# An encoder layer on one core: attention output stored in two halves, keys split over 128 partitions, value products recorded later

## The chip, the cores and the metric

One Trainium2 chip; the program runs on 1 of its cores. The metric is the device time of one execution in microseconds (us), lower is better. The engines are named as the profile names them: PE (TensorE) multiplies matrices, PEld is its weight load, ACT (ScalarE) and DVE (VectorE) work element by element, POOL (GpSimd) does a few small steps, SP (SyncE) issues every DMA. Each engine runs its own list of instructions in order and waits on semaphores.

## The reference, cut to what matters

One layer: three branches from one input projection, merged, then a feed-forward part with a convolution. Only the first branch is touched: stick-breaking attention, 16 heads of 64, 1024 prompt tokens and 64 sample tokens behind 256 cached ones, all float32.

```python
def _sb_block(qb, k, v, q_pos):
    mask = k_pos[None, :] < q_pos[:, None]
    z = einsum('bhqd,bhkd->bhqk', qb, k) * (SB_HEAD_DIM ** -0.5)
    log_beta = log_sigmoid(z)
    log_1mb = where(mask, log_sigmoid(-z), 0.0)
    excl = cumsum(log_1mb, axis=3, reverse=True) - log_1mb
    a = where(mask, exp(log_beta + excl), 0.0)
    return einsum('bhqk,bhkd->bhqd', a, v)
# in the layer
o_sb = stick_breaking(q, concat(k_past, k), concat(v_past, v), past_len)
y_sb = o_sb.transpose(0, 2, 1, 3).reshape(b, t, SB_WIDTH) @ w_sb_o
merged = sigmoid(ga) * y_sb + sigmoid(gb) * y_conv + sigmoid(gc) * y_mem
```

## The kernel before

Every large product keeps float32 accuracy with three passes of reduced-width matmuls: an operand x is split into a rounded part `hi` (written by ACT) and the rest `lo = x - hi` (written by DVE); `split` is these two instructions. Work runs in stages: memory keys and values; input projections with the convolution; then the attention stage of this case; three output projections (`mo` for memory, `cv` for convolution, `sb` for attention); the merged output projection; the feed-forward part.

**Attention stage.** Heads go in 8 pairs p = 0 to 7, a head of a pair is i = 0 or 1. `project(p)` makes q, k and v of a pair, each a dense product of 24 steps of three matmuls. Behind it runs the attention of pair p-1, cut into units: unit (p, i, c) holds queries 256c to 256c+255 (order c = 0, 2, 1, 3), and a sample unit closes each head. A unit makes scores `z` (PE, q in hi and lo against k stored as hi in 64 partitions and lo in the other 64), two sigmoids `be` and `r` (ACT), a scan of `r` and a product (DVE), and then for each block b of 256 keys a *turn* (four PE transposes into `aT`, split into `ath` by ACT and `atl` by DVE) and *values* (four matmuls of `ath` and `atl` against `vp`, whose 128 columns hold hi and lo of v). So one half of the 128 rows of the result `av` comes from v's hi part and the other from its lo part; their sum is the head's output. It is made here: ACT copies one half to `tmp` (L849), DVE adds the other to `os` (L851), and `os` goes to the DRAM tensor `d_os`.

**Order on PE.** PE's list is the order in which the code is recorded. `Weave.mix` lets one step of the projection pass and then asks `take` for a piece of attention that is due by a planner's clock `now`: values first (due 3.4 after their turn), then late transposes, turns, scores. No third turn is taken while two turned blocks wait for their values. At the start of `project(p)` for p > 1, `weave.until` records all that is left of pair p-2, due or not, piece after piece, with no projection step between. ACT, DVE and SP lists are set by a scheduler that places instructions by its own model. Buffers are handed out in the order of that model; `av` is one PSUM bank, `row` has four buffers.

**Output projection.** `project_out(1, ...)` runs `cv` for 8 column blocks m, then `project_out(0, ...)` runs `sb`. `sb` reads its operand as 8 rows of 128 channels: `sb_rows` loads rows 0 to 2 of `d_os` during the last `cv` block, the loop behind it the others; each is split into `sbh` and `sbl`. Block m = 0 of `sb` takes the 8 rows in turn, nine matmuls each. Gates (`cvg`, `sbg`) are loaded into the same four `row` buffers.

Of the kernel before, what the change touches and what calls it, by code (L numbers as in the profile page):

```python
# [8 lines left out]
F32 = mybir.dt.float32  # L9
F32R = mybir.dt.float32r  # L10
# [7 lines left out]
P = 128  # L18
# [32 lines left out]
def encoder_step(ctx: ExitStack, tc: tile.TileContext, I, O):  # L51
# [33 lines left out]
    d_silu = dp.tile([D, T], F32, name="d_silu")  # L85
    d_om = dp.tile([D, T], F32, name="d_om")
    d_os = dp.tile([D, T], F32, name="d_os")
    d_mg = dp.tile([D, T], F32, name="d_mg")
    d_x1 = dp.tile([T, D], F32, name="d_x1")

# [568 lines left out]
    with ExitStack() as st:  # L659
# [9 lines left out]
        def project(p, S):  # L669
# [62 lines left out]
            S["ks"], S["kc"] = ks, kc  # L732

            def k_split(dst, ps, c):
                for i in range(2):
                    a = slice(64 * i, 64 * i + 64)
                    b = slice(64 - 64 * i, 128 - 64 * i)
                    ACT.copy(out=dst[i][a, c], in_=ps[a, :])
                    DVE.tensor_tensor(out=dst[i][b, c], in0=ps[a, :], in1=dst[i][a, c].bitcast(F32), op=ALU.subtract)

            def evac_k(ps, t0, n):
                token_major(ps, t0, n, "k", O["sb_k_prompt"], O["sb_k_sample"])
# [39 lines left out]
        def unit(p, S, i, c):  # L782

            hr = slice(64 * i, 64 * i + 64)
            qd, ql, ks = S["qd"][i], S["ql"][i], S["ks"][i]
            bes, scores, rest = [], [], []

            def score(tb, gi, k0, m, cell):
                q = slice(tb * P, (tb + 1) * P)
                n = P * (tb + 1)  # L790
                if gi == 0:
                    tg = "s" if tb < 4 else ""
                    wd = 512 if tb < 4 else 1024
                    be = ap.tile([P, wd], F32, tag="be" + tg, name=f"be{p}{i}{tb}", bufs=4)
                    cell.append(ap.tile([P, wd], F32, tag="r" + tg, name=f"r{p}{i}{tb}", bufs=2))
                    bes.append(be)
                z = bank("z", f"z{p}{i}{tb}_{k0}")
                kk = slice(k0, k0 + m)
                PE.matmul(z[:, :m], qd[:, q], ks[:, kk], start=True, stop=False)
                dg = k0 <= tb * P < k0 + m  # L800
                PE.matmul(z[:, :m], ql[:, q], ks[:, kk], start=False, stop=not dg)
                if dg:
                    o = tb * P - k0
                    PE.matmul(z[:, o : o + P], identb, maskb, start=False, stop=True)
                be, r = bes[-1], cell[0]
                stick(P, [(z, k0, min(m, n - k0))], n, be, r)
                if k0 + m >= n:
                    sticks(P, n, be, r)

            for tb in (2 * c, 2 * c + 1):  # L810
                cell = []
                for gi, (k0, m) in enumerate(ZG[tb + 1]):
                    scores.append(lambda a=(tb, gi, k0, m, cell): score(*a))

            split_of = {}
            acc = []

            def turn(b):
                tp = bank("tr", f"aT{p}{i}{c}{b}")
                hi = ap.tile([P, 512], F32R, tag="ath", name=f"ath{p}{i}{c}{b}", bufs=2)  # L820
                lo = ap.tile([P, 512], F32R, tag="atl", name=f"atl{p}{i}{c}{b}", bufs=2)
                if b < c:
                    for a in range(2):
                        for e in range(2):
                            o = a * 256 + e * P
                            PE.transpose(tp[:, o : o + P], bes[e][:, (2 * b + a) * P : (2 * b + a + 1) * P], ident)
                    split(hi, lo, tp)
                    order = ((2 * b, 0, 0), (2 * b + 1, 0, 256))
                else:
                    PE.transpose(tp[:, 0:P], bes[1][:, (2 * c + 1) * P : (2 * c + 2) * P], ident)  # L830
                    for e in range(2):
                        PE.transpose(tp[:, (1 + e) * P : (2 + e) * P], bes[e][:, 2 * c * P : (2 * c + 1) * P], ident)  # L832
                    split(hi[:, 0:384], lo[:, 0:384], tp[:, 0:384])
                    order = ((2 * c, 0, P), (2 * c + 1, P, 0))
                split_of[b] = (hi, lo, order)

            def values(b):
                if b == 0:
                    acc.append(bank("av", f"av{p}{i}{c}"))
                av = acc[0]  # L840
                hi, lo, order = split_of.pop(b)
                for j, t0, o in order:
                    n = 256 - t0
                    PE.matmul(av[:, t0:256], S["vp"][i][:, j, :], hi[:, o : o + n], start=j == 0, stop=False)
                    PE.matmul(av[:, t0:256], S["vp"][i][:, j, :], lo[:, o : o + n], start=False, stop=j == 2 * c + 1)
                if b == c:
                    tmp = ap.tile([P, 256], F32, tag="tmp", name=f"tmp{p}{i}{c}", bufs=1)
                    ot = slice(64 - 64 * i, 128 - 64 * i)
                    ACT.copy(out=tmp[hr, :], in_=av[ot, :256])  # L849
                    os_ = ap.tile([P, 256], F32, tag="os", name=f"os{p}{i}{c}", bufs=2)  # L850
                    DVE.tensor_tensor(out=os_[hr, :], in0=av[hr, :256], in1=tmp[hr, :], op=ALU.add)  # L851
                    SP.dma_start(out=d_os[p * P + 64 * i : p * P + 64 * i + 64, 256 * c : 256 * c + 256], in_=os_[hr, :])

            n = P * (2 * c + 2)
            return Unit(scores, [lambda b=b: turn(b) for b in range(c + 1)], [lambda b=b: values(b) for b in range(c + 1)], n)
# [53 lines left out]
        class Weave:  # L909
# [23 lines left out]
            def take(self, force=False):  # L933

                if self.vq and (force or (self.vq[0][0] <= self.now and (self.vq[0][1] is self.summed or self.v_at + 2.6 <= self.now))):
                    _, u, f, last = self.vq.pop(0)
                    self.summed, self.v_at = u, self.now
                    f()
                    self.valued += 1
                    u.over = last  # L940
                    return self.PIECE
                if self.lq and (force or (self.lq[0][0] <= self.now and self.t_at[-2] + 2.6 <= self.now)):
                    self.lq.pop(0)[1]()
                    self.t_at.append(self.now)
                    return 0.33
                if self.tq and self.turned - self.valued < 2:
                    at, u, f, last = self.tq[0]
                    if force or (at <= self.now and self.t_at[-2] + 2.6 <= self.now):
                        self.tq.pop(0)
                        f()  # L950
                        self.t_at.append(self.now)
                        self.turned += 1
                        self.vq.append((self.now + 3.4, u, u.values[0], last))
                        u.values.pop(0)
                        if last:
                            self.done.append(u)
                        return self.PIECE
                if self.zq:
                    u, f, last = self.zq[0]
                    free = len(self.open) < 3 or u in self.open  # L960
                    if free and (force or (self.zq_ready <= self.now and self.z_at[-2] + 2.2 <= self.now)):
                        self.zq.pop(0)
                        if u not in self.open:
                            self.open.append(u)
                        f()
                        self.z_at.append(self.now)
                        if last:
                            for i, g in enumerate(u.turns):
                                self.tq.append((self.now + u.scan, u, g, i == len(u.turns) - 1))
                        return self.PIECE  # L970
                return 0.0
# [36 lines left out]

        def ap_tile(kind, shape, name):
            tag, bufs, w = {  # L1010
                "c": ("be", 4, 1024), "q": ("r", 2, 1024), "s": ("os", 2, 256), "v": ("tmp", 1, 256), "d": ("sf", 1, 192)
            }[kind]
            return ap.tile([P, w], F32, tag=tag, name=name, bufs=bufs)[:, : shape[1]]

# [123 lines left out]
    with ExitStack() as st:  # L1138
# [35 lines left out]

        sb_raw = []

        def sb_rows(m):
            if m == NK - 1:
                sb_raw.extend(row(d_os[k * P : (k + 1) * P, :], f"sbr{k}") for k in range(3))

        project_out(1, cv_ops, "cv", sb_rows, lambda m: None)
        sb_ops = act_rows("sb")
        for k in range(NK):
            raw = sb_raw[k] if k < len(sb_raw) else row(d_os[k * P : (k + 1) * P, :], f"sbr{k}")
            split(sb_ops[0][k], sb_ops[1][k], raw)
        project_out(0, sb_ops, "sb", lambda m: None, wo_load)

# [342 lines left out]
```

## Time and profile before

| | |
|---|---|
| median of 3 runs | 2532.03 us (2529.49 to 2532.94) |
| profiled execution | 2529.34 us, its span on the core 2527.5 us |
| PE busy | 2454.8 us, 97% of the span, 14639 matmuls |
| DVE busy / ACT busy | 1625.5 us (64%) / 1043.3 us (41%) |
| granted PE clock, mean | 0.998 |
| attention stage, 740 to 1380 us | PE busy 592.58 of 640 us, DVE 503.08, ACT 407.72 |
| DMA in all | 224.84 MB, mean 89 GB/s |

The span runs from the first to the last instruction; about 2 us of the execution lie around it. Since PE is busy nearly throughout and its list is fixed, the time is the sum of PE's work and of the stretches in which PE waits; the views that say where it waits are the table of waits by engine, the table of busy time by stage and the instructions in order of time.

### The profile page before, as it was taken

Reading aid. Unit: us, or ns where it says so; the run is one execution under the profiler, and the core shown is the slowest. Engines: PE = TensorE matmul, PEld = TensorE weight load, DVE = VectorE, ACT = ScalarE, POOL = GpSimd, SP = SyncE. Lnnn points to the kernel's source line nnn. Section 1 sums busy time; section 2 is a strip of 40 time slices with the busy share of each in tenths; the row PEclk is TensorE's granted clock in tenths of the full one; section 3 lists DMA queues with packets and bytes.
Section 4 is the critical chain, followed back from the end, with each engine's and each line's share of the span. In section 5 each row is a group of like instructions: output and inputs, shape, how many; then the busy total and the mean of one; then the engine's idle time right before and its main releaser. Section 6 shows DMA issues by size and latency. Waiting matters only on the chain. (4 is left out here: it accounts for less than half of the span.)

```text
span 2527.5 us, 36086 instructions
## 1 busy us (share of the span) xinstructions
PE 2454.8 (97%) x14639; PEld 2321.6 (92%) x14639; DVE 1625.5 (64%) x1963; ACT 1043.3 (41%) x2031; POOL 97.6 (4%) x301
## 2 busy tenths in 40 slices
PE   8999999999899999999989999999999999999998
PEld 6999999999898888888879999979999999999997
DVE  6687878787758777788786435444545444454456
ACT  7224142424656666566664203144223332222243
POOL 1000000000000000000000000011000000000001
PEclk9999999999999999999999999999999999999999
DMA  7322222222552322322343546122111110110114
GB/s 264 93 66 82 73 83 69 69 92 69 178 157 67 81 69 56 79 66 65 99 132 119 182 162 198 60 92 84 51 51 51 51 51 26 50 51 26 51 42 151
DMA packets 256055, 224.84 MB, mean 89 GB/s; under 512 B 58143, under 2 KB 227251, under 8 KB 255889
## 3 DMA queue, kind: packets, MB, share of 16 engines
q1 hardware_dynamic: 255889, 222.54, 29.3%
q8 instruction: 115, 1.88, 0.3%
q14 instruction: 51, 0.42, 0.1%
HBM read 153.22 MB, written 55.91 MB: 83 GB/s over the span
## 5 line engine op out<-in xcount | busy, mean ns | idle before, releaser
L93 DVE TENSOR_TENSOR wlo<-wraw,whi 128x1024 fp32r<-128x1024 f32 x156 | 190.3, 1220 | 280.5 <-ACT whi L92 277.9
L151 PE MATMUL up<-h2h,whi 128*128 128x362 f32 (+1 forms) x1056 | 348.2, 330 | 0.0
L152 PE MATMUL up<-h2l,whi 128*128 128x362 f32 (+1 forms) x1056 | 347.0, 329 | 0.0
L153 PE MATMUL up<-h2h,wlo 128*128 128x362 f32 (+1 forms) x1056 | 344.9, 327 | 0.0
L418 DVE SCALAR_TENSOR_TENSOR acc<-u,cw,acc 128x1118 f32<-128x1118 f32 x240 | 331.6, 1382 | 5.6
L92 ACT CAST whi<-wraw 128x1024 fp32r<-128x1024 f32 x156 | 164.3, 1053 | 302.3 <-PE cv L152 73.2
L1115 ACT COPY up<-up 128x364 f32<-128x364 f32 (+3 forms) x176 | 60.7, 385 | 352.0 <-PE up L153 352.0
L153 PEld LDWEIGHTS up<-h2h,wlo 128*128 128x128 f32 x1056 | 199.5, 189 | 0.0
L152 PEld LDWEIGHTS up<-h2l,whi 128*128 128x128 f32 x1056 | 198.6, 188 | 0.5
L151 PEld LDWEIGHTS up<-h2h,whi 128*128 128x128 f32 x1056 | 198.3, 188 | 0.4
L151 PE MATMUL g<-hh,whi 128*128 128x362 f32 (+1 forms) x576 | 190.4, 331 | 0.0
L153 PE MATMUL g<-hh,wlo 128*128 128x362 f32 (+1 forms) x576 | 189.2, 328 | 0.0
L152 PE MATMUL g<-hl,whi 128*128 128x362 f32 (+1 forms) x576 | 188.7, 328 | 0.0
L779 DVE TENSOR_TENSOR_SCAN r<-r 128x128 f32<-128x128 f32 (+7 forms) x128 | 171.8, 1350 | 25.4 <-ACT r L775 25.2
L1388 DVE TENSOR_TENSOR yacc<-yacc,dn 128x512 f32<-128x512 f32 x144 | 96.8, 686 | 82.6 <-PE dn L1375 62.2
L1107 DVE SCALAR_TENSOR_TENSOR fa<-up,fw,fa 128x1090 f32<-128x1090 f32 (+2 forms) x92 | 119.8, 1302 | 5.8 <-ACT fa L1105 4.5
L93 DVE TENSOR_TENSOR atl<-aT,ath 128x512 fp32r<-128x512 f32 (+1 forms) x160 | 99.0, 632 | 31.5 <-ACT ath L92 29.8
L92 ACT CAST ath<-aT 128x512 fp32r<-128x512 f32 (+1 forms) x160 | 85.6, 552 | 72.1 <-PE aT L832 39.2
L1375 PE MATMUL dn<-wdh,gl 128*128 128x512 f32 x288 | 112.2, 389 | 0.0
L1374 PE MATMUL dn<-wdl,gh 128*128 128x512 f32 x288 | 112.1, 389 | 0.0
L1373 PE MATMUL dn<-wdh,gh 128*128 128x512 f32 x288 | 112.1, 389 | 0.0
L152 PEld LDWEIGHTS g<-hl,whi 128*128 128x128 f32 x576 | 108.6, 189 | 0.2
(405 smaller groups left out, 6318.9 us busy)
## 6 DMA issues: line engine op xcount, KB each, us to landing
wraw<-in_w_in SPq DMA_DIRECT2D x72, 512.0 KB
wraw<-in_w_ffn_up SPq DMA_DIRECT2D x44, 512.0 KB
d_gate<-gt SPq DMA_DIRECT2D x24, 544.0 KB
wdr<-in_w_ffn_down SPq DMA_DIRECT2D x22, 512.0 KB
wraw<-in_w_mem_kv SPq DMA_DIRECT2D x16, 512.0 KB
qd<-qd SPq DMA_DIRECT2D x24, 272.0 KB
ql<-ql SPq DMA_DIRECT2D x24, 272.0 KB
d_om<-ost SPq DMA_DIRECT2D x8, 544.0 KB
```

The lines of the kernel that those rows point to most:

```text
L92: ACT.copy(out=hi, in_=src)
L93: DVE.tensor_tensor(out=lo, in0=src, in1=hi.bitcast(F32), op=ALU.subtract)
L151: PE.matmul(ps, wh[:, k, :], rh[k][c], start=first, stop=False)
L152: PE.matmul(ps, wh[:, k, :], rl[k][c], start=False, stop=False)
L153: PE.matmul(ps, wl[:, k, :], rh[k][c], start=False, stop=last)
L418: DVE.scalar_tensor_tensor(out=acc, in0=u[:, t : t + 1118], scalar=cw[:, t * 8 + i : t * 8 + i + 1], in1=acc, op0=ALU.mult, op1=ALU.add,)
L779: DVE.tensor_tensor_scan(out=rv, data0=rv, data1=rv, initial=1.0, op0=ALU.mult, op1=ALU.min)
L1107: DVE.scalar_tensor_tensor(out=acc[:, a:b], in0=raw[:, a + t : b + t], scalar=fw[:, t * 44 + m : t * 44 + m + 1], in1=acc[:, a:b], op0=ALU ...
L1373: PE.matmul(y, gh[:, tt], wh[:, c], start=first, stop=False)
L1374: PE.matmul(y, gh[:, tt], wl[:, c], start=False, stop=False)
L1375: PE.matmul(y, gl[:, tt], wh[:, c], start=False, stop=last)
L1388: DVE.tensor_tensor(out=yacc[t][:, c], in0=yacc[t][:, c], in1=y, op=ALU.add)
```

## The change

Five edits, all around the attention stage.

1. **Output halves.** The add in the values step goes. ACT copies all 128 rows of `av` into `os` (L853 of the changed kernel), and two DMAs store the halves, one to `d_os`, one to a new DRAM tensor `d_ol`. When `sb` needs a row, `sb_row` loads it from both and DVE adds them (L1185). The second load takes a `row` buffer too, and two rows instead of three are loaded ahead.
2. **Key split.** `k_split` was two ACT copies and two DVE subtractions on 64 partitions each. It is now one `split` on 128 partitions, and three DMAs per chunk that carry the halves to their places. The third overwrites what the second reads.
3. **Values later.** The planner's delay from a turn to its values goes from 3.4 to 4.6.
4. **Buffers.** `be` of the long score rows: four buffers of 1024 become one of each width (640, 768, 896, 1024); `r`: two of 1024 become one of 896 and one of 1024.
5. **Layer norm tiles** of the one block (64 rows) left for this stage take the renamed buffers.

```diff
+    d_ol = dp.tile([D, TP], F32, name="d_ol")
             def k_split(dst, ps, c):
-                for i in range(2):
-                    a = slice(64 * i, 64 * i + 64)
-                    b = slice(64 - 64 * i, 128 - 64 * i)
-                    ACT.copy(out=dst[i][a, c], in_=ps[a, :])
-                    DVE.tensor_tensor(out=dst[i][b, c], in0=ps[a, :], in1=dst[i][a, c].bitcast(F32), op=ALU.subtract)
+                n = c.stop - c.start
+                hi = ap.tile([P, 384], F32R, tag="kh", name=f"kh{p}_{n}_{c.start}", bufs=3)
+                split(hi[:, :n], dst[1][:, c], ps)
+                up, dn = slice(0, 64), slice(64, P)
+                for out, src in ((dst[0][up, c], hi[up, :n]), (dst[0][dn, c], dst[1][up, c]), (dst[1][up, c], hi[dn, :n])):
+                    SP.dma_start(out=out.bitcast(F32), in_=src.bitcast(F32))
...
-                    be = ap.tile([P, wd], F32, tag="be" + tg, name=f"be{p}{i}{tb}", bufs=4)
-                    cell.append(ap.tile([P, wd], F32, tag="r" + tg, name=f"r{p}{i}{tb}", bufs=2))
+                    else:
+                        be = ap.tile([P, n], F32, tag=f"be{tb}", name=f"be{p}{i}{tb}", bufs=1)
+                        cell.append(ap.tile([P, P * (7 + tb % 2)], F32, tag=f"r{tb % 2}", name=f"r{p}{i}{tb}", bufs=1))
...
                 if b == c:
-                    tmp = ap.tile([P, 256], F32, tag="tmp", name=f"tmp{p}{i}{c}", bufs=1)
-                    ot = slice(64 - 64 * i, 128 - 64 * i)
-                    ACT.copy(out=tmp[hr, :], in_=av[ot, :256])
                     os_ = ap.tile([P, 256], F32, tag="os", name=f"os{p}{i}{c}", bufs=2)
-                    DVE.tensor_tensor(out=os_[hr, :], in0=av[hr, :256], in1=tmp[hr, :], op=ALU.add)
-                    SP.dma_start(out=d_os[p * P + 64 * i : p * P + 64 * i + 64, 256 * c : 256 * c + 256], in_=os_[hr, :])
+                    ACT.copy(out=os_, in_=av[:, :256])
+                    rows = slice(p * P + 64 * i, p * P + 64 * i + 64)
+                    for h, dst in enumerate((d_os, d_ol)):
+                        SP.dma_start(out=dst[rows, 256 * c : 256 * c + 256], in_=os_[64 * h : 64 * h + 64, :])
...
-                        self.vq.append((self.now + 3.4, u, u.values[0], last))
+                        self.vq.append((self.now + 4.6, u, u.values[0], last))
...
+        def sb_row(k):
+            raw = row(d_os[k * P : (k + 1) * P, :], f"sbr{k}")
+            low = op.tile([P, T], F32, tag="row", name=f"sbl{k}", bufs=4)
+            SP.dma_start(out=low[:, :TP], in_=d_ol[k * P : (k + 1) * P, :])
+            DVE.tensor_tensor(out=raw[:, :TP], in0=raw[:, :TP], in1=low[:, :TP], op=ALU.add)
+            return raw
...
-                sb_raw.extend(row(d_os[k * P : (k + 1) * P, :], f"sbr{k}") for k in range(3))
+                sb_raw.extend(sb_row(k) for k in range(2))
...
-            raw = sb_raw[k] if k < len(sb_raw) else row(d_os[k * P : (k + 1) * P, :], f"sbr{k}")
+            raw = sb_raw[k] if k < len(sb_raw) else sb_row(k)
```

How the lists move, at three places. A row names line, operation, output and inputs; in `aT2133` the digits are pair 2, head 1, unit 3, block 3, and `v3_2` is the third chunk of v of pair 3.

**PE, where the projections of pair 4 begin.** Before, the end of unit (2, 1, 3): steps of `v3_2` stand between a turn and its values, 20 rows from `aT2133` to `ath2133`.

```order
L830 MATMUL aT2133_9426<-ident_69,be217_9174 128x128
...
L153 MATMUL v3_2_9434<-hh3_113,wlo75_8878 128x320
L844 MATMUL av213_9385<-ath2132_9409,vp21_8310 128x256
...
L151 MATMUL v3_2_9434<-hh4_114,whi75_8877 128x320
...
L844 MATMUL av213_9385<-ath2133_9427,vp21_8310 128x256
...
L893 MATMUL avs21_9496<-sf21_9455,vpr2_7948 128x64 x2
L894 MATMUL avs21_9496<-sf21_9455,vn0_6354 128x64
L151 MATMUL q4_0_9509<-hh0_110,whi76_9230 128x384
```

Now the same place: v has ended, and what is left of the unit follows in one piece.

```order
L154 MATMUL v3_2_9392<-hh7_118,wlo75_8886 128x320
L849 MATMUL av213_9457<-ath2130_9397,vp21_8288 128x256
...
L831 MATMUL aT2132_9462<-ident_69,be217_9222 128x128
L849 MATMUL av213_9457<-ath2131_9417,vp21_8288 128x256
...
L849 MATMUL av213_9457<-ath2132_9463,vp21_8288 128x256
...
L706 MATMUL vT3_768_9483<-ident_69,vf3_768_9455 128x128 x2
...
L835 MATMUL aT2133_9499<-ident_69,be217_9222 128x128
...
L849 MATMUL av213_9457<-ath2133_9500,vp21_8288 128x256
...
L885 MATMUL asT21_9515<-ident_69,bes21_9304 128x128 x3
L897 MATMUL avs21_9521<-sf21_9519,vpr2_7956 128x64 x2
...
L152 MATMUL q4_0_9534<-hh0_111,whi76_9250 128x384
```

What moved: the values of blocks 1, 2 and 3 and of the sample, and the turns of blocks 2 and 3, from between steps of `v3` to behind its last one; block 2's values now have only block 1's between them and their turn, block 3's nothing. The same stands at the starts of `q2` to `q7`, six times; for pairs 0, 4 and 5 block 1's values have only block 0's between them and their turn as well, for pair 3 a step of v besides.

**ACT at the same place.** Before:

```order
L92 CAST ath2132_9409<-aT2132_9408 128x512
L699 COPY vf3_384_9420<-v3_1_9326 128x384
L92 CAST ath2133_9427<-aT2133_9426 128x384
L883 COPY sf21_9455<-asT21_9451 128x192
L849 COPY tmp213_9464<-av213_9385 64x256
L710 COPY vs3_384_9473<-vT3_384_9469 128x384
L92 CAST vp30_9228<-vT3_384_9469 128x3x64
L92 CAST vp31_9229<-vT3_384_9469 128x3x64
L699 COPY vf3_768_9490<-v3_2_9434 128x320
L92 CAST whi77_9503<-wraw77_9234 128x1024
L896 COPY oss21_9500<-avs21_9496 64x64
```

Now:

```order
L700 COPY vf3_768_9455<-v3_2_9392 128x320
L93 CAST whi77_9528<-wraw77_9254 128x1024
L93 CAST vp31_9249<-vT3_384_9440 128x3x64
L93 CAST ath2132_9463<-aT2132_9462 128x512
L711 COPY vs3_768_9487<-vT3_768_9483 128x256
L93 CAST vp30_9248<-vT3_768_9483 128x2x64
L93 CAST ath2133_9500<-aT2133_9499 128x384
L93 CAST vp31_9249<-vT3_768_9483 128x2x64
L721 COPY vs3_768_9487<-vT3_768_9483 64x128
L853 COPY os213_9511<-av213_9457 128x256
L887 COPY sf21_9519<-asT21_9515 128x192
L900 COPY oss21_9525<-avs21_9521 64x64
```

What moved: `ath2132` and `ath2133` stood ahead of the copies of v's last chunks and of the weight split `whi77`, which cannot start before v has ended; now they stand behind them.

**SP, the loads for `sb`.** Before (`wraw` and `wor` are weights, `sbg` gates):

```order
L1144 DMA sbr0_15174<-d_os_100 128x1088
L124 DMA wraw105_15184<-in_w_sb_o 128x8x128
L1144 DMA sbr1_15176<-d_os_100 128x1088
L124 DMA wraw106_15315<-in_w_sb_o 128x8x128
L1144 DMA sbr2_15178<-d_os_100 128x1088
L1172 DMA wor0_15398<-in_w_out 128x1024
L1144 DMA sbr3_15289<-d_os_100 128x1088
L1144 DMA sbr4_15293<-d_os_100 128x1088
L1144 DMA sbr5_15297<-d_os_100 128x1088
L124 DMA wraw107_15408<-in_w_sb_o 128x8x128
L1144 DMA sbr6_15301<-d_os_100 128x1088
L1144 DMA sbr7_15305<-d_os_100 128x1088
```

Now:

```order
L1148 DMA sbr0_15175<-d_os_100 128x1088
...
L1184 DMA sbl0_15177<-d_ol_101 128x1024
...
L1148 DMA sbr1_15180<-d_os_100 128x1088
L1184 DMA sbl1_15182<-d_ol_101 128x1024
L1176 DMA wor0_15423<-in_w_out 128x1024
L1148 DMA sbr2_15292<-d_os_100 128x1088
L1184 DMA sbl2_15294<-d_ol_101 128x1024
...
L1184 DMA sbl3_15301<-d_ol_101 128x1024
L1148 DMA sbr4_15306<-d_os_100 128x1088
...
L1184 DMA sbl7_15329<-d_ol_101 128x1024
...
L1148 DMA sbg0_15334<-d_gate0_94 128x1088
```

What moved: each of the eight rows is two loads, so the places that were taken by rows 1 and 2 while `cv` was still running are taken by the second half of row 0 and by row 1. A load waits until its buffer is free: `sbl1` for the end of the next to last `cv` block, `sbl2` for the add of row 1, `sbr3` for row 1's split, `sbl3` for the add of row 2, `sbl5` for row 3's split, `sbl7` for row 5's split.

More of the change, by code (lines that the diff above doesn't have):

```diff
@@ L791, in score @@
                 if gi == 0:
-                    tg = "s" if tb < 4 else ""
-                    wd = 512 if tb < 4 else 1024
-                    be = ap.tile([P, wd], F32, tag="be" + tg, name=f"be{p}{i}{tb}", bufs=4)
-                    cell.append(ap.tile([P, wd], F32, tag="r" + tg, name=f"r{p}{i}{tb}", bufs=2))
+                    if tb < 4:
+                        be = ap.tile([P, 512], F32, tag="bes", name=f"be{p}{i}{tb}", bufs=4)
+                        cell.append(ap.tile([P, 512], F32, tag="rs", name=f"r{p}{i}{tb}", bufs=2))
+                    else:
+                        be = ap.tile([P, n], F32, tag=f"be{tb}", name=f"be{p}{i}{tb}", bufs=1)
+                        cell.append(ap.tile([P, P * (7 + tb % 2)], F32, tag=f"r{tb % 2}", name=f"r{p}{i}{tb}", bufs=1))
                     bes.append(be)
@@ L1010, in ap_tile @@
             tag, bufs, w = {
-                "c": ("be", 4, 1024), "q": ("r", 2, 1024), "s": ("os", 2, 256), "v": ("tmp", 1, 256), "d": ("sf", 1, 192)
+                "c": ("be7", 1, 1024), "q": ("r1", 1, 1024), "s": ("os", 2, 256), "v": ("os", 2, 256), "d": ("sf", 1, 192)
             }[kind]
```

## The prediction

> **What bounds the kernel now.** I read the page's busy times, then busy time by stage, then PE's waits, then the instructions around them.
>
> ```profile
> PE 2454.8 (97%) x14639; PEld 2321.6 (92%) x14639; DVE 1625.5 (64%) x1963; ACT 1043.3 (41%) x2031; POOL 97.6 (4%) x301
> 740.00:1380.00 640.00, 592.58 (x3990) 551.38 (x3989) 503.08 (x700) 407.72 (x962) 0.54 (x1) 1.00 0.33 85
> 1380.00:1520.00 140.00, 140.00 (x849) 140.00 (x847) 52.58 (x76) 21.20 (x20) 0.00 (x0) 1.00 0.48 164
> 1520.00:1560.00 40.00, 40.00 (x245) 40.00 (x243) 28.31 (x36) 15.03 (x15) 0.00 (x0) 1.00 0.75 250
> PE av L845 <- DVE atl L93: 26.7, 23, 1.7
> PE z L799 <- ACT r L775: 10.0, 8, 1.3
> PE av L844 <- DVE os L851: 4.9, 9, 1.1
> PE vT L705 <- DVE vp L93: 3.3, 1, 3.3
> PE avs L893 <- DVE os L851: 1.3, 1, 1.3
> ```
>
> Columns of the stages: length, then busy time of PE, PEld, DVE, ACT, POOL, then clock and DMA. PE is the bound: it idles 47.4 us in the attention stage and not at all from 1380 on, where `cv` and `sb` run. The change leaves PE's matmuls as they are, so only waits count: it can win at most those of the attention stage, and whatever it makes PE wait after 1380 us is new. All five waits listed (total, times, longest) fall in that stage; four of them, 42.9 us, are what the change reaches.
>
> **The change part by part: the waits it removes.** The largest is for `atl`, the rest of a turned block. It comes 3 times per head pair, here the longest; and the wait of `z` is one stall of ACT:
>
> ```profile
> 859.98 0.39 PE L845 MATMUL av<-atl,vp 128*128 128x256 f32 x1 [1.64 <-DVE atl L93]
> 884.18 0.55 DVE L739 TENSOR_TENSOR ks<-k,ks 64x384 fp32r<-64x384 f32 x1
> 884.77 0.47 ACT L738 CAST ks<-k 64x384 fp32r<-64x384 f32 x1 [1.22 <-DVE ks L739]
> 885.71 0.54 ACT L775 ACTIVATE r<-z 128x448 f32<-128x448 f32 x1
> 886.30 0.50 PE L799 MATMUL z<-ks,qd 128*128 128x512 f32 x1 [1.30 <-ACT r L775]
> ```
>
> Values move 1.2 later: waits of up to 1.2 vanish, the one per pair of up to 1.7 keeps 0.4, so of 26.7 some 3.4 stay. The second key copy on ACT waited 1.22 for DVE's subtraction, and everything behind it on ACT, the sigmoid that frees a `z` bank among it, came late. One split on 128 partitions has no such wait: 10.0 goes. `av` now waits only for ACT's copy, not for DVE's add behind it: 4.9 goes, and 1.3 may return as ACT's queue. Sum: 38 won. Ends: all 43; or 33, if `atl` keeps 5 more because DVE's scans land elsewhere. ACT and DVE lose the old copies and adds (64 adds and half of the key work); they do not bound, so that counts only through these waits.
>
> What is free: 96 key copies and 64 stores of `d_ol` on SP, whose list has room. SP blocks until the second key copy has landed before it issues the third; behind it wait weight loads, which run two blocks ahead, and the stores of `os`. The cover of the keys is the whole v projection, 72 matmuls. If a blocked SP holds `os` back, ACT's next copy waits: up to 1 us per pair, 8 in all, kept for the upper end. Buffer names and layer norm tiles: the same rotation (units take widths 640 to 1024 in turn), nothing.
>
> **The waits it adds in the attention stage.** By the order, the rest of a pair is now recorded in one piece before `q2` to `q7`. A turn's way through ACT and DVE, and what stands in the queues:
>
> ```profile
> 831.21 0.60 PE L826 MATMUL aT<-ident,be 128*128 128x128 f32 x4
> 831.56 0.42 PE L151 MATMUL v<-hh,whi 128*128 128x384 f32 x1
> 831.89 0.58 ACT L92 CAST ath<-aT 128x512 fp32r<-128x512 f32 x1
> 832.17 0.28 PE L844 MATMUL av<-ath,vp 128*128 128x256 f32 x1
> 832.51 0.69 DVE L93 TENSOR_TENSOR atl<-aT,ath 128x512 fp32r<-128x512 f32 x1 [0.33 <-ACT ath L92]
> 832.64 0.27 PE L830 MATMUL aT<-ident,be 128*128 128x128 f32 x1
> 832.89 0.39 PE L151 MATMUL v<-hh,whi 128*128 128x320 f32 x1
> 833.22 0.48 ACT L92 CAST ath<-aT 128x384 fp32r<-128x384 f32 x1 [0.36 <-PE aT L832]
> L92 ACT CAST whi<-wraw 128x1024 fp32r<-128x1024 f32 x156 | 164.3, 1053 | 302.3 <-PE cv L152 73.2
> L93 DVE TENSOR_TENSOR wlo<-wraw,whi 128x1024 fp32r<-128x1024 f32 x156 | 190.3, 1220 | 280.5 <-ACT whi L92 277.9
> L849 ACT COPY tmp<-av 64x256 f32<-64x256 f32 x48 | 17.6, 366 | 19.4 <-PE av L845 18.8
> L883 ACT COPY sf<-asT x16: 318/318/321, 801.3 to 1371.7; 128x192 f32<-128x192 f32 x16
> ```
>
> A turn of four transposes holds PE 0.35 (831.21 to 831.56), its `atl` is there at 833.20, 1.99 after its start. Four value matmuls hold PE 0.47; the second of them is the first that needs `atl`. With only block 1's values between, PE is there after 0.35 + 0.47 + 0.11 = 0.93: it waits 1.06. Block 3 (three transposes, 0.25, nothing between): `ath` ends 833.70 and about 0.55 for `atl` make 1.6 after its start; PE is there after 0.36 and waits 1.25. The sample: its transposes, then `os` (0.37) and `sf` (0.32) on ACT: 0.75. That is 3.1 per flush on empty queues, one more block (1.06) for pairs 0, 4 and 5, half of one for pair 3: 3 x 3.1 + 0.5 + 3 x 4.1 = 22 for six flushes, the lower end.
>
> The queues are not empty. ACT's list has `vf` (about 0.43) and `whi` (1.05) behind v's last matmul, then `ath2132`; DVE has `wlo` (1.22) ahead of `atl`. From v's end: 0.25 + 0.43 + 1.05 + 1.22 + a `vp` (0.36) + 0.69 = 4.0; PE gets there at 0.47 + 0.35 + 0.47 + 0.11 = 1.4 and waits 2.6, not 1.06. Block 3 stands behind two copies of v's last chunk: 1.55. Then 0.75. Together 4.9 (pairs 1 and 2), about 5.4 (pair 3), 6.1 (pairs 0, 4, 5): 33.5, and some 1 us where pair 6's last turns are taken without a projection beside them. I take 34, since the order shows these queues; the upper end is 40, with one more 1.2 behind a `wlo` per flush.
>
> **The wait it adds at `sb`.** Before, the loads just keep up:
>
> ```profile
> 1520.34 0.32 SPq L1144 DMA_DIRECT2D sbr<-d_os  x1
> 1524.45 1.10 ACT L92 CAST sbh<-sbr 128x1088 fp32r<-128x1088 f32 x1 [1.17 <-DMA sbr<-d_os]
> 1530.65 1.78 SPq L1144 DMA_DIRECT2D sbr<-d_os  x2
> 1530.90 0.33 PE L151 MATMUL sb<-sbh,whi 128*128 128x364 f32 x1
> 1532.38 0.33 PE L151 MATMUL sb<-sbh,whi 128*128 128x364 f32 x1
> 1536.05 1.10 ACT L92 CAST sbh<-sbr 128x1088 fp32r<-128x1088 f32 x1 [2.16 <-DMA sbr<-d_os]
> 1539.53 1.28 DVE L93 TENSOR_TENSOR sbl<-sbr,sbh 128x1088 fp32r<-128x1088 f32 x1
> L1237 DVE TENSOR_TENSOR xr<-xr,tt x9: 1206/1218/1226, 1640.8 to 1734.7; 128x1024 f32<-128x1024 f32 x8, 64x1024 f32<-64x1024 f32 x1
> ```
>
> PE takes a row every 1.48 us from 1530.90, so it needs the rest of row 7 at 1530.90 + 7 x 1.48 + 0.16 = 1541.4; it was ready at 1540.81. A load takes 4.1 (1520.34 to 1524.45) to 5.4 (1530.65 to 1536.05), a cast 1.1, a subtraction 1.3, an add of this size 1.2. Now the chain of buffers: `sbl1` starts at 1520.3, when the next to last `cv` block ends; it lands after 4.1; add of row 1, then `sbl2`; add of row 2, then `sbl3`; add and split of row 3, then `sbl5`; add and split of row 5, then `sbl7`. Five loads (4.1 + 4 x 4.75 = 23.1), four adds (4.9), two splits (4.8): `sbl7` is there at 1553.1; row 6's subtraction ends about 1553.3; add and split of row 7 take 3.6: 1556.9. PE waits 15.5, say 16. Nothing later takes it back, since PE never idles there. With 4.1 a load DVE's own order holds the end at about 1554.5 (13); with 5.4 it is 19.
>
> The Trainium skill, "DMA: Bandwidth & Descriptors" (how a DMA's cost splits into fixed and variable parts), gives about 2.0 us plus bytes over 436 GB/s, an estimate of 3.2 us for such a load; by it the wait would be about 13. The loads here take longer, with DMA at 0.75 of its time between 1520 and 1560, so the rows decide.
>
> **Sum.** -38 + 34 + 16 = +12 us on the profiled execution's 2529.3, whose span is 2527.5: 2541.3. That execution lies 2.7 below the median of the runs, so 2544.
>
> **The rivals.**
>
> 1. *Empty queues, faster.* ACT and DVE have less to do, so the flushes cost their bare 22 and every listed wait goes: -43 + 22 + 16 = -5, 2527. It decides when a flush costs below 17 / 6 = 2.8 us with 38 won. For it: before, the same blocks get their `atl` 1.4 after their turn ended. Against: `whi`, `wlo` and the copies of v stand ahead of them in the lists. 0.13.
> 2. *No difference.* The `sb` loads turn out hidden: -38 + 34 + 0 = -4, 2528; or half hidden. Against: the lists make each half wait for the add before it. 0.17.
> 3. *The clock falls as well.* PE's one long wait is followed by a lower granted clock:
>
> ```profile
> 1302.79 0.65 PE L705 MATMUL vT<-ident,vf 128*128 128x128 f32 x2 [3.28 <-DVE vp L93]
> 1300.00:1305.00 5.00, 2.21 (x9) 2.25 (x10) 4.35 (x10) 3.92 (x11) 0.00 (x0) 0.78 0.90 261
> 1305.00:1310.00 5.00, 5.00 (x30) 4.57 (x28) 3.22 (x6) 2.85 (x8) 0.00 (x0) 0.88 0.57 158
> ```
>
> The clock was 0.78 and 0.88 in these ten us: 5 x 0.22 + 5 x 0.12 = 1.7 us of full-speed work lost. A flush has 5 us of waits within 8, in pieces of 1 to 3; if each is answered so, six flushes and the `sb` wait cost 7 x 1.7 = 12 more: 2556. Against: no single piece of a flush reaches 3.28. 0.20. The Trainium skill, "TensorE: Matmul & The Clock Gate" (Part 1 and its section on HAM oscillation), says that PE's clock falls to half after an idle window of about 3.4 us and takes as long to come back; the 3.28 us wait agrees.
>
> 4. *Later is not enough.* DVE's scans move along with the turns and the `atl` waits stay: only 16 won, +34, 2566. Against: `atl` came at most 1.7 late. 0.05.
>
> **How the numbers follow.** The likeliest, 0.45, is the sum, its own range 2534 to 2554 (two of the three terms at their ends). 8 in 10 reach from 2528, where rival 2 lies, to 2560, above rival 3. 0.2% is 5 us, about what a measurement of this kernel can tell. Faster takes rival 1, 0.13, and a little of 2: 0.15. Within 5 us: the rest of 2 and the sum's low edge, 0.18. Slower: 0.67.
>
> **What would show it.** In the changed profile PE's waits for `atl` between the pairs are gone, and `z` no longer waits for `r` once per pair; at six places, 76 us apart, PE waits three or four times within 8 us, for `atl` and for `sf`; the matmuls of the first `sb` block wait about 16 us in all, for `sbh` and `sbl`, and DVE's adds of L1185 wait for DMA. I am wrong if the flush places wait under 3 us each, or if `sb`'s first block takes 12 us as before.

## The result, and the profile after

The changed kernel takes 2555.75 us (median of 4 runs, 2555.59 to 2558.93), the kernel before 2532.1 on the same chip: by the means of the runs 1.0098 times as long, 95% interval 1.0081 to 1.0116. The forecast of a loss holds; its size, 12 us, is half of the measured 24. The profiled execution took 2555.68 us with a span of 2553.9, so the spans differ by 26.4 us.

PE's row of the busy times of the changed kernel says where to look: the same 14639 matmuls, and 31 us more of busy time.

```profile
PE 2485.8 (97%) x14639; PEld 2348.9 (92%) x14639; DVE 1588.8 (62%) x1875; ACT 1022.1 (40%) x1999; POOL 97.3 (4%) x301
```

To compare stages that start at different times, each kernel's trace is cut at its own first matmul of `q`, of `cv`, of `sb` and of the product after `sb`. Busy time by stage, first the kernel before, then the changed one (length, busy time of PE, PEld, DVE, ACT and POOL, granted clock, DMA):

```profile
723.79:1435.79 712.00, 664.58 (x4424) 623.38 (x4423) 527.83 (x729) 422.13 (x979) 0.54 (x1) 1.00 0.35 91
1435.79:1530.90 95.11, 95.11 (x579) 95.11 (x577) 42.75 (x62) 17.38 (x17) 0.00 (x0) 1.00 0.56 189
1530.90:1626.00 95.10, 95.10 (x578) 95.10 (x577) 48.91 (x71) 18.75 (x18) 0.00 (x0) 1.00 0.44 142
```

```profile
725.08:1445.24 720.16, 686.72 (x4424) 644.89 (x4424) 482.08 (x633) 401.16 (x947) 0.54 (x1) 0.96 0.41 107
1445.24:1540.96 95.72, 95.72 (x578) 95.72 (x578) 43.38 (x62) 13.80 (x14) 0.00 (x0) 1.00 0.56 192
1540.96:1652.52 111.56, 102.02 (x577) 98.70 (x577) 57.76 (x79) 22.17 (x21) 0.00 (x0) 0.94 0.48 156
```

The attention stage is 8.2 us longer, `sb` 16.5, `cv` 0.6, and what lies ahead 1.3. In the attention stage PE waits less than before (720.16 - 686.72 = 33.4 us against 47.4); what grew is its busy time, at a granted clock of 0.96. PE's waits, in the form of the prediction's list:

```profile
PE av L849 <- ACT ath L93: 9.0, 14, 1.0
PE av L850 <- DVE atl L94: 6.9, 16, 1.0
PE sb L152 <- ACT sbh L93: 5.9, 2, 3.9
PE sb L153 <- DVE sbl L94: 3.5, 6, 0.9
PE avs L897 <- ACT sf L887: 2.5, 6, 0.4
```

The regular waits for `atl` and the `z` wait are gone. The flushes, as the forced pieces ahead of `q2` to `q7` are called here, stand where the order put them. These are the 13.5 us ahead of each (length, PE's busy time, clock, DMA):

```profile
832.12:845.62 13.50, 9.59 (x45) 0.67 0.36 92
909.00:922.50 13.50, 10.86 (x79) 0.98 0.42 106
985.00:998.50 13.50, 10.43 (x65) 0.82 0.40 101
1065.50:1079.00 13.50, 9.73 (x52) 0.75 0.37 95
1143.80:1157.30 13.50, 10.12 (x59) 0.88 0.41 102
1222.30:1235.80 13.50, 10.12 (x59) 0.88 0.41 102
```

PE waits 2.6 to 3.9 us in each, 20.2 in all, and the clock is below 1 in every one. The lost clock is seen best at the first, ahead of `q2`. The clock records of the trace change only at moments 3.41 us, or a whole number of times that, apart; these windows are cut there (third column: PE's busy time; the clock is the last but two):

```profile
829.79:833.20 3.41, 3.35 (x28) 3.10 (x26) 1.05 (x2) 1.93 (x5) 0.00 (x0) 1.00 0.09 20
833.20:836.62 3.42, 1.49 (x10) 1.29 (x11) 2.09 (x3) 1.61 (x4) 0.00 (x0) 1.00 0.40 96
836.62:840.03 3.41, 2.54 (x11) 1.84 (x9) 1.27 (x4) 1.55 (x5) 0.00 (x0) 0.50 0.86 229
840.03:843.44 3.41, 2.78 (x12) 2.08 (x11) 0.69 (x2) 0.64 (x2) 0.00 (x0) 0.50 0.05 12
843.44:846.86 3.42, 3.01 (x13) 2.61 (x12) 0.00 (x0) 0.74 (x3) 0.00 (x0) 0.50 0.17 41
846.86:850.27 3.41, 3.41 (x14) 3.22 (x13) 1.83 (x4) 1.10 (x4) 0.00 (x0) 0.50 0.19 43
850.27:853.69 3.42, 3.42 (x23) 3.16 (x22) 1.11 (x1) 1.64 (x5) 0.00 (x0) 1.00 0.00 0
```

Between 833.20 and 836.62 PE was busy 1.49 of 3.42 us, 44%. From the end of that stretch the clock is half, for four stretches, until one in which PE is busy throughout. The same place instruction by instruction, PE alone:

```profile
834.38 0.39 PE L849 MATMUL av<-ath,vp 128*128 128x256 f32 x1 [1.24 <-ACT os L853]
836.00 0.39 PE L850 MATMUL av<-atl,vp 128*128 128x256 f32 x1 [0.75 <-DVE atl L94]
838.75 0.58 PE L849 MATMUL av<-ath,vp 128*128 128x256 f32 x1 [0.73 <-ACT ath L93]
841.75 0.58 PE L849 MATMUL av<-ath,vp 128*128 128x256 f32 x1 [0.62 <-ACT ath L93]
844.31 1.12 PE L897 MATMUL avs<-sf,vpr 128*128 128x64 f32 x4 [0.41 <-ACT sf L887]
845.62 0.67 PE L152 MATMUL q<-hh,whi 128*128 128x384 f32 x1
```

No wait is longer than 1.24 us, and together they are 3.8. The first wait, 1.24, is for ACT's copy of the unit before out of `av`, which stands behind `whi` on ACT; the prediction had no such wait. Yet the matmul of `q` at 845.62, behind the last of them, takes 0.67 at half clock; at full clock, in the run e1 below, the same one takes 0.42:

```profile
846.08 0.42 PE L152 MATMUL q<-hh,whi 128*128 128x384 f32 x1
```

The attention stage holds 18 such half-clock stretches. PE is busy 55.6 us in them, so at half speed some 28 us of work are lost (an estimate: half of that busy time). 15 of the 18 lie at the six flushes, with 46.2 us of busy time and so some 23 lost; the other three are elsewhere, one behind a single wait of 1.62 at 809.3 and two at a wait of 2.19 at 1307.7. The kernel before had one such stretch.

At `sb` PE starts at 1540.96 and needs the rest of row 7 at 1540.96 + 7 x 1.48 + 0.16 = 1551.5. DVE's last subtraction there:

```profile
1566.03 1.29 DVE L94 TENSOR_TENSOR sbl<-sbr,sbh 128x1088 fp32r<-128x1088 f32 x1 [1.21 <-ACT sbh L93]
```

It ends at 1567.32, 15.8 late. The list of waits shows only 9.4 us of this: the clock was half for 4 stretches there too, and a slower PE waits less.

### The profile page after: what moved, and what is told of

Same layout as the page of the kernel before. It is cut to its first block, busy times and chain, and to the rows that moved or that the text cites. A ratio compares the mean times of both kernels' runs of the same rounds, so it can differ in the third digit from the quotient of the medians.

```text
span 2553.9 us, 36210 instructions
## 1 busy us (share of the span) xinstructions
PE 2485.8 (97%) x14639; PEld 2348.9 (92%) x14639; DVE 1588.8 (62%) x1875; ACT 1022.1 (40%) x1999; POOL 97.3 (4%) x301
## 5 line engine op out<-in xcount | busy, mean ns | idle before, releaser
L777 ACT ACTIVATE be<-z 128x128 f32<-128x128 f32 (+2 forms) x192 | 97.8, 509 | 39.8 <-PE z L806 25.9
```

What stands on the lines that cost most here:

```text
L777: ACT.activation(be[:rows, c0 : c0 + m], zt[:rows, :m], AF.Sigmoid, scale=0.125)
```

## Experiments

All runs were timed against the kernel before on the same chip; a ratio is that of the mean times, with its 95% interval. "Half clock" counts the 3.41 us stretches at half clock. The stage columns come from one execution of each run, and the kernel before, run beside the experiments, took 2529.1 to 2537.3 us, so a difference of 2 or 3 us between two stages says little.

| run | us | ratio | attention stage, us | PE idle in it | half clock in it | `sb` stage, us |
|---|---|---|---|---|---|---|
| before | 2532.1 | | 712.0 | 47.4 | 1 | 95.1 |
| changed | 2555.75 | 1.0098 (1.0081 to 1.0116) | 720.2 | 33.4 | 18 | 111.6 |
| e1_fill | 2549.64 | 1.0067 (1.0050 to 1.0084) | 712.5 | 24.4 | 5 | 113.2 |
| e2_q_late | 2508.44 | 0.9904 (0.9889 to 0.9919) | 669.0 | 15.4 | 1 | 113.7 |
| e3_delay34 | 2521.77 | 0.9958 (0.9943 to 0.9973) | 683.5 | 25.3 | 2 | 111.2 |
| e4_one_store | 2560.09 | 1.0107 (1.0086 to 1.0127) | 744.0 | 45.2 | 24 | 95.7 |
| e5_key_only | 2520.5 | 0.9958 (0.9943 to 0.9973) | 702.4 | 40.0 | 3 | 95.1 |
| e6_q_late_one_store | 2509.89 | 0.9915 (0.9898 to 0.9931) | 690.4 | 26.4 | 3 | 95.1 |
| e7_add_by_dma | 2500.6 | 0.9879 (0.9864 to 0.9894) | 680.5 | 21.5 | 2 | 95.1 |
| e8_add_two_copies | 2503.91 | 0.9892 (0.9877 to 0.9906) | 683.6 | 23.9 | 2 | 95.1 |
| e9_before_delay | 2555.91 | 1.0095 (1.0080 to 1.0110) | 737.0 | 47.6 | 18 | 95.7 |
| e10_before_delay_q_late | 2517.71 | 0.9942 (0.9927 to 0.9957) | 698.9 | 31.1 | 6 | 95.1 |
| e11_five_rows | 2500.65 | 0.9877 (0.9860 to 0.9893) | 671.2 | 12.8 | 4 | 106.0 |
| e12_sb_fill | 2506.55 | 0.9899 (0.9884 to 0.9914) | 671.3 | 13.1 | 4 | 113.2 |

Two theories stood after the first comparison. The clock theory: what the flushes cost is mostly the clock, which is halved when PE is busy too little in a 3.4 us stretch. The rival: they cost the time that PE waits there, and the clock follows something else. The first experiments' sizes, 19.7 us of waits and 15 stretches at the flushes, come from the changed trace.

**e1_fill: more work at the flushes.** `fill` is 6 in the call at the start of `project(p)`, 0 elsewhere.

```diff
             def until(self, cond, fill=0):
                 while not cond():
+                    turns = len(self.t_at)
                     self.now += self.take(force=True) or 0.46
+                    if fill and len(self.t_at) > turns:
+                        ps = bank("mm", f"fill{turns}")
+                        for e in range(fill):
+                            PE.matmul(ps[:, :384], hT[0][0][:, 0:P], hT[0][e % NK][:, 0:384], start=e == 0, stop=e == fill - 1)
```

> The changed kernel with extra work: each time a turn or a late transpose is recorded in the forced piece at the starts of q2 to q7, six matmuls of 128x384 on the normalized input follow it, into a spare bank that nothing reads. They add about 0.96 us of PE work per place, 3 or 4 places per flush, some 20 us in all. Clock theory: the changed kernel lost its time because PE's share of busy time in single 3.4 us stretches at the flushes fell so low that the clock was halved for 15 such stretches (25.6 us); with PE kept busy that halving goes, waits of about 13 of the 19.7 us are covered by the added work, and the time falls in spite of the added work, to about 2537. Rival (the flush costs only the time PE waits, the clock follows something else): no gain from the clock, at best the added work hides in the waits, 2556 to 2564.

It added 132 matmuls and became 6 us faster than the changed kernel. Its windows around the flush ahead of `q2`, cut at its own clock stretches:

```profile
833.93:837.35 3.42, 1.81 (x12) 1.61 (x13) 2.09 (x3) 1.29 (x4) 0.00 (x0) 1.00 0.35 84
837.35:840.76 3.41, 3.41 (x14) 3.31 (x13) 0.81 (x3) 1.65 (x5) 0.00 (x0) 0.50 0.90 233
840.76:844.17 3.41, 3.37 (x22) 2.92 (x22) 1.25 (x2) 0.48 (x1) 0.00 (x0) 1.00 0.02 5
```

The same waits as before it drop the clock, since the first fill stands behind them; but with PE kept busy it is back after one stretch, not four. Over the stage 18 half-clock stretches became 5 and idle time fell by 9 us, against some 21 us of added work (132 at about 0.16). The rival can't explain that extra work shortens the program, nor that the clock comes back where nothing but PE's busy share was raised. The gain is smaller than expected (2549.6 against 2537): 9 us of waits were covered, not 13, two flushes still lost the clock for a stretch each, three half stretches elsewhere stayed, and `sb` took 1.6 us more.

**e2_q_late: the same pieces between steps of q.** Where the diff has "...", the tiles `qd` and `ql` are taken, as before at the start.

```diff
             def evac_q(ps, t0, n):
-                c = slice(t0, t0 + n)
-                split(qd[0][:, c], ql[0][:, c], ps)
-            if p > 1:
-                weave.until(lambda: all(u.over for u in weave.units[p - 2]))
+                held.append((ps, slice(t0, t0 + n)))
+                if len(held) < 2 and not qd:
+                    return
+                if not qd:
+                    if p > 1:
+                        weave.until(lambda: all(u.over for u in weave.units[p - 2]))
...
+                while held:
+                    ps, c = held.pop(0)
+                    split(qd[0][:, c], ql[0][:, c], ps)
```

> The changed kernel with the forced recording moved from the start of q of a pair to the end of its second chunk (the tiles of q are taken there, and the first chunk is evacuated there too). The rest of a pair's values is then recorded between steps of q, with 3.4 us or more between a turn and its values. Clock theory: the six flushes' waits (19.7 us) and their 15 half clock stretches (25.6 us) go: about 2512, PE waits in the attention stage about 15 us, no granted clock under 1 there but near 1300. Rival (waits alone): 2536 to 2540. By the prediction's own size of a flush, 34 us without any clock: 2522.

Its attention stage and its `sb`:

```profile
726.96:1395.94 668.98, 653.59 (x4425) 622.76 (x4423) 480.15 (x633) 399.62 (x947) 0.54 (x1) 1.00 0.44 116
1491.05:1604.71 113.66, 105.35 (x578) 102.00 (x577) 57.55 (x78) 21.93 (x21) 0.00 (x0) 0.89 0.47 152
PE av L856 <- DVE atl L94: 1.6, 5, 0.4
1516.36 1.29 DVE L94 TENSOR_TENSOR sbl<-sbr,sbh 128x1088 fp32r<-128x1088 f32 x1 [1.21 <-ACT sbh L93]
```

47 us under the changed kernel, close to the 43 expected, and but for one half stretch, as in the kernel before, the clock in the stage is whole again. The flushes therefore cost 720.2 - 669.0 = 51.2 us of the stage: 18.0 less idle time, 33.1 less busy time for the same matmuls. The half-clock stretches account for some 26 of the 33 (27.8 us of work lost in the changed kernel; 1.5 here, half of the 3.0 us that PE is busy in its one); some 7 are left over.

**e3_delay34: the delay back at 3.4.** One number in the line that queues the values, 4.6 to 3.4.

> The changed kernel with the delay from a turn to its values back at 3.4. The flushes go (the order at the starts of q2 to q7 is that of the kernel before), and the waits of av for atl come back. Clock theory: 2555.8 - 19.7 (flush waits) - 25.6 (clock) + 26 (waits for atl, 23 times up to 1.7) = about 2537. Rival (waits alone): 2562. By the prediction's sizes: 2555.8 - 34 + 23 = 2545.

15 us better than either theory said. The waits for `atl` came back, though smaller than in the kernel before (26.7):

```profile
PE av L850 <- DVE atl L94: 21.2, 23, 1.3
725.23:1408.72 683.49, 658.22 (x4423) 625.21 (x4423) 479.62 (x633) 401.11 (x947) 0.54 (x1) 1.00 0.43 113
```

The flushes gave back 51 us (e2), not the 45 of the expectation, and the shorter delay cost 14.5 (683.5 - 669.0), not 26. Net, the delay with its flushes costs 720.2 - 683.5 = 36.7 us.

**e4_one_store: output added before it is stored**, as in the kernel before (the diff of the output and of `sb_row` undone; `kh` with two buffers for room).

> The changed kernel with the output added before it is stored, as in the kernel before (ACT copies one half, DVE adds the other, one store, one load per row of sb); to make room the tile for the rounded keys has two buffers instead of three. The waits at the first sb block (9.3 us) go and with them three half clock stretches (5.1 us); waits of av for os return, 4.9 us, and may add to a flush. About 2546. By the prediction's size of the sb wait (16): 2545. Rival (the sb wait comes from DMA load at this place, not from the second load and the add): 2556.

`sb` is back at 95.7, as expected. But the total missed the 2546 expected, because the attention stage lost 24 us: `av` and `avs` wait for the add on DVE again. Waits of `av` of 2.73 ahead of `q2` and of 1.51 ahead of `q6` and of `q7` are at flushes, where the add stands on DVE behind `wlo`; those of `avs` are elsewhere.

```profile
PE avs L897 <- DVE os L855: 8.7, 8, 3.7
PE av L848 <- DVE os L855: 8.4, 7, 2.7
722.89:1466.87 743.98, 698.76 (x4423) 651.25 (x4423) 504.95 (x697) 405.75 (x947) 0.54 (x1) 0.94 0.37 98
```

So the new output path is worth 24 us of attention stage here, 11.8 of them idle time; the clock, with 24 half stretches instead of 18, shares in the rest.

**e5_key_only: the key split and the buffers alone** (e4 with the delay at 3.4).

> Of the change, the key split on 128 partitions and the smaller score buffers alone: delay 3.4, output added before it is stored, one load per row of sb (tile for rounded keys with two buffers). From the run with the delay at 3.4 (2521.8): the late sb rows go (row 7 about 12 to 13 us late there, some clock besides: 14), av waits for os come back (5 to 6): 2513. If the key split and the buffers were worth only the prediction's 10 us of z waits: 2532 - 10 = 2522.

It matches the prediction's term, not my later estimate: the attention stage is 9.6 us shorter than before, the `z` wait is gone, and the waits for `atl` grew by 3.3.

```profile
PE av L849 <- DVE atl L93: 30.0, 23, 1.6
PE z L803 <- ACT r L777: 0.7, 1, 0.7
725.63:1428.01 702.38, 662.38 (x4425) 626.41 (x4424) 507.39 (x697) 407.68 (x947) 0.54 (x1) 0.99 0.39 104
```

Between this run and e3 only the output path (and one buffer of `kh`) differs: it wins 702.4 - 683.5 = 18.9 us in the attention stage and gives back 16.1 at `sb`.

**e6 to e8: the moved piece, and the add in other places.** e6 is e2 with the old add. e7 adds in the attention stage behind ACT's copy:

```diff
                     ACT.copy(out=os_, in_=av[:, :256])
-                    for h, dst in enumerate((d_os, d_ol)):
-                        SP.dma_start(out=dst[rows, 256 * c : 256 * c + 256], in_=os_[64 * h : 64 * h + 64, :])
+                    SP.dma_start(out=tmp, in_=os_[64:P, :])
+                    DVE.tensor_tensor(out=os_[0:64, :], in0=os_[0:64, :], in1=tmp, op=ALU.add)
+                    SP.dma_start(out=d_os[rows, 256 * c : 256 * c + 256], in_=os_[0:64, :])
```

e8 has two ACT copies onto the same partitions instead of the copy and the DMA. `sb` is loaded as in the kernel before in all three, and the tile for the rounded keys has two buffers instead of three.

> The run with q's forced piece moved (2508.4) with the output added before it is stored: the late rows at sb go (14), waits of av and avs for os return. If these are as before (6 us): 2500. If they are as with the flushes (17 us in the run with one store): 2511.

> The run with q's forced piece moved, and the two halves added in the attention stage behind ACT's copy: ACT copies av into os, a DMA brings the lower half to the upper partitions, DVE adds, one store, one load per row of sb. av waits for ACT alone, sb for one load: 2508.4 - 14 = 2494; up to 3 more if DVE's adds or os (two buffers, held over a DMA of some 2 us) make ACT's copies late: 2497.

> As the run before it, but ACT copies the two halves one after the other onto the same partitions and DVE adds them there, no DMA between. av is free after two copies (0.37 us each) instead of one and never waits for DVE: 2494, plus 0.2 to 0.4 us where av waits for ACT already: up to 2498.

e6 met its higher figure: the old add costs 21 us of stage even without flushes, of which 11.0 are idle time, mostly where the sample's `avs` follows a unit at once:

```profile
PE avs L903 <- DVE os L861: 12.4, 12, 3.7
```

e7 and e8 have no wait of `av` for DVE's add, keep `sb` at 95.1 and are faster than the kernel before by 1.2% and 1.1%. They lie 4 and 6 us above the upper ends expected: their attention stage is 12 and 15 us longer than that of e2, of which 6 to 8.5 are idle time. Whether the third buffer of the keys has a part in that was not tried.

**e9 and e10: the delay in the kernel before.** e9 changes the one number, 3.4 to 4.6; e10 also moves the forced piece as in e2.

> The kernel before with the delay from a turn to its values at 4.6 and nothing else. If the loss belongs to the delay, with the forced piece and the clock behind it, it comes here as well: between the runs with one store the delay alone cost 2560.1 - 2520.5 = 39.6, so 2530 + 40 = 2570, with 15 to 20 half clock stretches behind the pairs. If it needs the changed output or keys: under 2540. By the prediction's sizes (34 for the forced pieces, 23 won at atl): 2541.

> The kernel before with the delay at 4.6 and the forced piece moved to the end of q's second chunk; keys and output as before. The waits for atl (26.7) go, those for os and z stay and may grow, no flush, no half clock: 2530 - 24 + 0 to 6 = 2506 to 2512. If the gain of the moved piece needs the new key split: 2520 or more.

```profile
722.41:1459.45 737.04, 689.47 (x4424) 642.99 (x4423) 525.20 (x729) 418.34 (x979) 0.54 (x1) 0.96 0.33 88
725.78:1424.71 698.93, 667.80 (x4424) 629.11 (x4423) 524.95 (x729) 417.65 (x979) 0.54 (x1) 0.99 0.35 93
```

One number makes the kernel before 24 us slower, as slow as the whole change, at the same clock of 0.96: the loss belongs to the delay. My figure, 14 us higher, was the step from e5 to e4; why the delay costs 41.6 us of stage there and 25.0 here stays open. e10 is 38 us better than e9 and gains without the new keys and output; it stays nearly 6 us above its range, with 18 us of waits for `os`.

**e11 and e12: what sets the time at `sb`.** e11 is e2 with `bufs=5` for `row`; e12 is e2 with six extra matmuls ahead of each of rows 1 to 7.

> The run with q's forced piece moved (2508.4), with five row buffers instead of four around the output projections. If the late rows at sb come from the chain of buffers (a load waits for a buffer that an add or a split has to free), one buffer more takes about one load of 4 to 5 us off the chain: 2504. If they come from what the DMA queues can move there, no change: 2508.

> The run with q's forced piece moved (2508.4), with six extra matmuls of 128x384 on the weights, into a spare bank that nothing reads, ahead of each of rows 1 to 7 of the first sb block (some 6.9 us of PE work). If the 7 half clock stretches there cost what they look like (12 us), filling the waits saves most of it: 2498 to 2501. If the rows' arrival sets the time and the slow clock only fills what would be waiting, filling saves just the tail behind row 7: 2505 to 2508.

Their `sb` stages and DVE's last subtractions there (rows 7), e11 and then e12:

```profile
1491.61:1597.60 105.99, 99.91 (x577) 97.59 (x577) 55.34 (x77) 21.05 (x20) 0.00 (x0) 0.97 0.45 150
1509.21 1.29 DVE L94 TENSOR_TENSOR sbl<-sbr,sbh 128x1088 fp32r<-128x1088 f32 x1 [1.49 <-ACT sbh L93]
```

```profile
1492.40:1605.64 113.24, 107.28 (x620) 105.37 (x619) 57.46 (x78) 22.02 (x21) 0.00 (x0) 0.97 0.48 154
1517.85 1.29 DVE L94 TENSOR_TENSOR sbl<-sbr,sbh 128x1088 fp32r<-128x1088 f32 x1 [1.21 <-ACT sbh L93]
```

One more buffer brings row 7 from 16.1 late (e2: ready 1517.65, needed 1501.5) to 1510.50 - 1502.13 = 8.4: the chain of buffers sets it, and e11 becomes as fast as e7. Filling PE's waits leaves row 7 16.2 late and the stage where it was, although the clock was halved for 2 stretches instead of 7. Here the slow clock is nearly free: PE would have waited in any case.

## Why the prediction was right on the sign and wrong on the size

| term | predicted | measured | from |
|---|---|---|---|
| attention waits removed | -38 | -43.0 | stage of e2 against before |
| of it, keys | -10.0 | -9.6 | e5 against before |
| of it, `av` free after ACT's copy | -5 | -18.9 | e3 against e5 |
| of it, later values, without flushes | -23 | -14.5 | e2 against e3 |
| the six flushes | +34 | +51.2 | changed against e2 |
| `sb` | +16 | +16.5 | stage of changed against before |
| ahead of the stage, and at `cv` | 0 | +1.9 | rows of the stages |

The sum of the measured terms is +26.6, against 26.4 between the spans.

**The step that failed is "the waits it adds in the attention stage".** It priced a flush by the time PE waits and left the clock to a rival. Both halves were off, in opposite directions. The waits are 18.0 us by e2 (20.2 in the six windows), under the 22 for empty queues, not 34. At the flush ahead of `q2`, priced at 6.1, they are 3.8: 1.24 and 0.75 behind the turn of block 1, the first behind v's end, not 2.6; 0.73 and 0.62 behind blocks 2 and 3, at half clock, the latter not 1.55; 0.41 at the sample, not 0.75. The rest, 33 us, is the same matmuls taking longer, some 26 of it by the halved clock. The prediction's own sign of being wrong, flushes that wait under 3 us each, was met at one of the six (2.6).

**Rival 3 named the mechanism and mis-sized it.** It read the clock as the answer to one long wait ("no single piece of a flush reaches 3.28") and charged 1.7 us per flush. The traces show that the busy share of a whole stretch counts, that two waits of 1.24 and 0.75 within one suffice, and that the clock stays down for up to four: some 23 us at the six flushes, not 10. That its time, 2556, agrees with the measurement is luck: at the flushes its waits were 16 us too long and its longer busy time 23 us too short (33 against 10), and the waits removed were 5 us more than it said.

**The waits removed** were right in sum by two errors that cancel in part. The `z` term was right. Copying `av` out with ACT alone brought 18.9, not 5; 30.0 of `atl` waits became 21.2 with it. That DVE, with 64 adds less in its queue, reaches `atl` sooner fits this but was argued only. The -14.5 is that of the delay with the forced piece moved out of the way. Of the 43.0, 32.0 is idle time; 11.0 is busy time of the same matmuls at the same clock. The first matmul behind a wait stands longer in the trace (0.39 against 0.28 for `av`), so a wait costs more than its listed time; that this is all of the 11, or of the 7 left over in e2, wasn't tried.

**`sb` was right**, 15.8 late against 15.5, and by its own chain: one buffer more shortens it. The listed waits there are 9.4, not the 16 foretold, because the slower PE fills the rest: it is busy 102.0 us there against 95.1. The Trainium skill's figure for a load ("DMA: Bandwidth & Descriptors", fixed and variable parts), which the page fits to another way of issuing, from GpSimd, gave 13; the rows' own durations were nearer.

Rivals 1 and 2 fall: flushes did cost more than 2.8 us, and the `sb` loads weren't hidden. Rival 4 falls: with the flushes out, 1.6 us of `atl` waits of `av` are left in e2.

## What to carry to other kernels

Where PE is the bound, look for places where several short waits fall within 3 to 4 us, not only for the longest wait: there the clock may cost more than the waits, as extra busy time, and even useless matmuls can pay. A point that forces out leftover work, because a buffer is taken early, is the place to look at when a delay is raised: taking the buffer later, between steps of the next product, was worth 47 us here. Where PE waits for data in any case, the slow clock costs little, and the chain of buffers is the thing to shorten.

## What the chip showed that was not expected

- In the fourteen profiles, the first and last 17 us left out, the clock goes from full to half 69 times, each time at the end of a 3.41 us stretch of a fixed grid. In 66 of them PE was busy at most 55% of that stretch, at most 62% in the others. 24 stretches of 46 to 55% kept the full clock; none under 45% did. The edge is near one half, and a few tenths of a microsecond decide, or where the grid happens to lie: a wait of `avs` of 1.62 near 808 us left one stretch 53% busy in the changed kernel and halved the clock, while in e2 the same wait fell on two stretches, 87% and 65% busy, and did not.
- It comes back only at the end of a stretch in which PE was busy 87% or more; stretches of up to 96% still kept it at half. So a flush, whose later waits keep PE below that, costs up to four stretches.
- The Trainium skill, "TensorE: Matmul & The Clock Gate" (Part 1, and the table on why this matters for kernels), has the same 3.4 us grid and the two clocks, and asks for no idle gap over about 3 us. The measurement differs from that advice: at the flush above the longest gap is 1.24 us, and the clock is halved.
